# Rows of cumulative exponents for SSD heads: from selection matmuls to broadcast transfers, in a hybrid encoder

## The chip, the cores and the metric

The kernel runs on one core of one Trainium2 chip. The metric is the device time in microseconds; shown is the median of several executions. One further execution was recorded by the hardware profiler, and all durations come from that one.

## The reference

A two-layer encoder works on 16 meta tokens and 512 tokens of 2048 channels (528 positions). The first layer projects to SSD heads (Mamba-2, run in both directions) and to a convolution branch, gates both and projects back; the second is neighbourhood attention. The change lies in the SSD heads. Cut to one direction of them:

```python
A_cs = jnp.cumsum(A, axis=2)                     # per chunk and head, A = dt * -exp(A_log)
seg = A_cs[:, :, :, None] - A_cs[:, :, None, :]
Lmat = jnp.exp(jnp.where(tri, seg, -jnp.inf))
CB = jnp.einsum("bclgn,bcsgn->bclsg", Cc, Bc)
Y_diag = jnp.einsum("bclsgr,bcsgrp->bclgrp", CB[..., None] * Lmat, X)
...
Y_off = jnp.einsum("bclgn,bcgrpn->bclgrp", Cc, prev) * jnp.exp(A_cs)[..., None]
return (Y_diag + Y_off)
```

There are 32 heads of 64 channels in 8 groups; a group shares Bm and Cm. For each head and direction the kernel needs the row of cumulative exponents A_cs over all positions on many partitions at once: once as it is, to form the differences `seg` in a chunk, and once as exp(A_cs), to scale Cc for the part that comes from earlier chunks.

## The kernel before

Activations lie with channels on partitions and the 528 positions along the free dimension (L = 528, HL = 264). Positions are cut into NC = 6 chunks of CH = 88.

Every projection (`proj`) multiplies in three passes of 32-bit parts (high x high, high x low, low x high): for each of the 16 slices of the inner dimension 3 passes x 2 halves of 264 columns, 96 matmuls for a tile of 128 output channels. Weight panels of half a tile (128 x 8 x 128) are loaded on SP's queue (`load`), cast to the high part by ACT (L256, `wh`), subtracted to the low part by DVE (L259, `wl`); `raw`, `wh` and `wl` have three buffers each. The results lie in the PSUM tile `ps` (two buffers) and are taken out by DVE.

For each of the 8 groups, one or two further tiles of the convolution branch are projected (`glu_tile`), then six tiles: Bm (`bT`), Cm (`cT`), two of xs, two of z. After each projection `step()` lets two background generators go on: `ssd` of the group before, by a budget of 7000, and the 31-tap convolutions (`conv31`, on DVE, L447), by 6000. Each `yield` in a generator is the price of what it just emitted, and is taken off the budget. The tile framework then orders the instructions of each engine ahead of the run by a model of their times; the program order acts as priority. A fixed order of each engine results.

Ahead of the first group, `fc` is computed: 64 partitions (2 directions x 32 heads) x 528 cumulative exponents, from two scans (L514, L515). It is split into a high and a low part, both in `fhl` (128 partitions, L516 to L518). `sel` is a constant 128 x 64 of zeros and ones. dt and its relatives lie in slots that T and cq use afterwards (L486). Transposed columns of fc, dt and the decay to a chunk's end are in `fcol`, `dcol`, `wcol` (L535 to L542).

`ssd` of one group, in order: products of chunk and chunk (`pc`, L550) and their two masked forms (`cbs`); for each chunk the transposes (L563), the decayed inputs (`xd`) and the states (`st`, L573, into `pv`); the running states (L582, L585); then for each of two pairs of heads (`i`), for each head (`j`):

- for each direction, two matmuls (L598) with one column of `sel` spread over 128 columns select the row of fc for this head and put it on all 128 partitions in the PSUM tile `pf`;
- ACT forms T = relu(fcol - row) in six blocks of 88 columns (L601) and cq = exp(row) (L603), then T = exp(-T) (L604);
- DVE multiplies cq by cT (L605, L606); ACT scales T by dcol (L611), DVE multiplies by `cbs` (L612) and adds the directions (L614).

Both heads of a pair then go into `py` (L633), 64 matmuls from T, cq, xb and pv in six chunks; DVE takes it out (L637), multiplies by the gate (L638), and POOL's queue stores it to `yz_d` (L639). T and cq have two buffers each, so one pair of heads fills them. pc, pf and py share one slot of two PSUM banks (tag "big").

POOL's own work in this stage is small: the memsets at the edges of the convolution input `up` (L459, L460), one multiplication for each `glu_tile` (L656), the stores of `yz_d` and `cv_d`. Its instructions and the transfers on its queue run in order.

The next stage (from L706) projects 16 more tiles with `ln` beside it, then come the output projection, the attention layer and the last output projection, all with the same weight path.

Of the kernel before, what the change touches and what calls it, by code (L numbers as in the profile page):

```python
# [12 lines left out]
F32 = mybir.dt.float32  # L13
F32R = mybir.dt.float32r
AF = mybir.ActivationFunctionType
ALU = mybir.AluOpType

P = 128
# [5 lines left out]
L = NM + S  # L24
HL = L // 2
# [4 lines left out]
HPG = 4  # L30
HD = 64
CH = 88
NC = L // CH
NH = 32
# [48 lines left out]
def hybrid_encoder(ctx: ExitStack, tc: tile.TileContext, hT, win, wdt, wout, oin, oout, par, con,  # L83
                   rpb, out, dbg=None):
    nc = tc.nc
    dbg = dbg or {}

    cp = ctx.enter_context(tc.tile_pool(name="cp", bufs=1))
# [3 lines left out]
    dr = ctx.enter_context(tc.tile_pool(name="dr", bufs=1, space=bass.MemoryType.DRAM))  # L92
# [15 lines left out]
    def cn(n):  # L108
        lo, hi = CON[n]
        return cst[:, lo:hi]  # L110
# [4 lines left out]
    def h2(ap):  # L115
        return ap.rearrange("p (a b) -> p a b", a=2)

    yz_d = dr.tile([KT, P, L], F32, name="yz_d")
    cv_d = dr.tile([KT, P, L], F32, name="cv_d")
    pt_d = dr.tile([KT, P, L], F32, name="pt_d")  # L120
    yb_d = dr.tile([KT, P, L], F32, name="yb_d")
# [252 lines left out]
    with ExitStack() as c0:  # L374
        psb = c0.enter_context(tc.tile_pool(name="psb", bufs=1, space=bass.MemoryType.PSUM))
        sp = c0.enter_context(tc.tile_pool(name="sp", bufs=1))
        dp = c0.enter_context(tc.tile_pool(name="dp", bufs=1))
# [13 lines left out]
        for tag, n, bufs in (("T", 2, 2), ("T", 2, 2), ("cq", 2, 2), ("cq", 2, 2), ("xb", 4, 1), ("pv", 4, 1)):  # L391
            t = first_x if not raws else sp.tile([P, n, L], F32, name="hraw", tag=tag, bufs=bufs)
            for i in range(n):
                k = len(raws)
# [17 lines left out]
                if k >= 2:  # L412
                    nc.vector.tensor_tensor(ac, ac, raw, op=ALU.add)

        sel = cp.tile([P, 64], F32R, name="sel")
        nc.vector.tensor_copy(sel, cn("sel"))
        xp = [sp.tile([P, L + 4], F32, name=f"xp{i}") for i in range(2)]
        for t in xp:
            nc.gpsimd.memset(t[:, 0:2], 0.0)
# [2 lines left out]
        J = 64  # L422
# [64 lines left out]
        v, e, w, z, la, fc, wd, dexp = [t4[i // 2][:J, i % 2] for i in range(8)]  # L487
# [25 lines left out]
        nc.gpsimd.memset(rf[:, ::CH], 0.0)  # L513
        nc.vector.tensor_tensor_scan(fc[0:32], rf[0:32], la[0:32], 0.0, ALU.mult, ALU.add)  # L514
        nc.vector.tensor_tensor_scan(fc[32:64, ::-1], rf[32:64], la[32:64, ::-1], 0.0, ALU.mult, ALU.add)  # L515
        fhl = dp.tile([P, L], F32R, name="fhl")  # L516
        nc.scalar.activation(fhl[:J], fc, AF.Copy)
        nc.vector.tensor_tensor(fhl[J:], fc, fhl[:J].bitcast(F32), op=ALU.subtract)  # L518
        fc3 = fc.rearrange("p (c t) -> p c t", c=NC)
        wd3 = wd.rearrange("p (c t) -> p c t", c=NC)  # L520
        nc.vector.tensor_tensor(wd3[0:32], fc3[0:32, :, CH - 1:CH].to_broadcast([32, NC, CH]), fc3[0:32], op=ALU.subtract)
# [14 lines left out]
        for nm, src in (("fcol", fc), ("dcol", dt), ("wcol", wd)):  # L536
# [3 lines left out]
            t = dp.tile([CH, NC, 2, NH], F32, name=nm)  # L540
            nc.vector.tensor_copy(t.rearrange("p c r h -> p (c r h)"), pt[:CH, :NC * J])
            cols.append(t)  # L542
        fcol, dcol, wcol = cols

        def ssd(g, bT, cT, xs, zs):
            xb = sp.tile([CH, NC, 3 * P], F32, name="xb", tag="xb")
            pv = sp.tile([P, NC - 1, 2, 256], F32, name="pv", tag="pv")
            pc = psb.tile([P, 2, 512], F32, name="pc", tag="big")
# [11 lines left out]
            for c in range(NC):  # L560
                pt = psb.tile([P, 512], F32, name="pt", tag="sm", bufs=2)
                for i, src in enumerate((xs[0], xs[1], bT)):
# [11 lines left out]
                                 start=True, stop=True)  # L574
# [12 lines left out]
            for i in range(2):  # L587
                gs, cs = [], []
                for j in range(2):
                    hl = 2 * i + j  # L590
                    hd = HPG * g + hl
                    T = sp.tile([CH, 2, L], F32, name="T", tag="T", bufs=2)
                    cq = sp.tile([P, 2, L], F32, name="cq", tag="cq", bufs=2)
                    for d in range(2):
                        pf = psb.tile([P, 2, 512], F32, name="pf", tag="big")
                        jj = d * NH + hd
                        for n in range(2):
                            nc.tensor.matmul(pf[:, n, :HL], sel[:, jj:jj + 1].to_broadcast([P, P]),  # L598
                                             fhl[:, n * HL:(n + 1) * HL], start=True, stop=True)
                        for c in range(NC):  # L600
                            nc.scalar.activation(T[:, d, c * CH:(c + 1) * CH], pf[:CH, c // 3, (c % 3) * CH:(c % 3 + 1) * CH],  # L601
                                                 AF.Relu, bias=fcol[:, c, d, hd:hd + 1], scale=-1.0)
                        nc.scalar.activation(h2(cq[:, d]), pf[:, :, :HL], AF.Exp)  # L603
                    nc.scalar.activation(T, T, AF.Exp, scale=-1.0)  # L604
                    nc.vector.tensor_tensor(cq[:, 0, CH:], cq[:, 0, CH:], cT[:, CH:], op=ALU.mult)  # L605
                    nc.vector.tensor_tensor(cq[:, 1, :L - CH], cq[:, 1, :L - CH], cT[:, :L - CH], op=ALU.mult)  # L606
                    yield 1050
                    for d in range(2):
                        for c in range(NC):
                            sl = slice(c * CH, (c + 1) * CH)  # L610
                            nc.scalar.activation(T[:, d, sl], T[:, d, sl], AF.Copy, scale=dcol[:, c, d, hd:hd + 1])  # L611
                        nc.vector.tensor_tensor(T[:, d], T[:, d], cbs[d], op=ALU.mult)  # L612
                    yield 1900
                    nc.vector.tensor_tensor(T[:, 0], T[:, 0], T[:, 1], op=ALU.add)  # L614
                    yield 650
                    gs.append(T)
                    cs.append(cq)
                py = psb.tile([P, 2, 512], F32, name="py", tag="big")
                for c in range(NC):
                    sl = slice(c * CH, (c + 1) * CH)  # L620
                    terms = [[], []]
                    for j in range(2):
                        hs = slice((2 * i + j) * HD, (2 * i + j + 1) * HD)
                        terms[j].append((xb[:, c, hs], gs[j][:, 0, sl]))
                        if c > 0:
                            terms[j].append((pv[:, c - 1, 0, hs], cs[j][:, 0, sl]))
                        if c < NC - 1:
                            terms[j].append((pv[:, NC - 2 - c, 1, hs], cs[j][:, 1, sl]))
                    nt = len(terms[0])
                    for q in range(nt):  # L630
                        for j in range(2):
                            a, b = terms[j][q]
                            nc.tensor.matmul(py[j * HD:(j + 1) * HD, c // 3, (c % 3) * CH:(c % 3 + 1) * CH], a, b,  # L633
                                             start=(q == 0), stop=(q == nt - 1))
                ti = 2 * g + i
                y = xs[i]
                nc.vector.scalar_tensor_tensor(h2(y), h2(y), pr("dd", ti, ti + 1), py[:, :, :HL], op0=ALU.mult, op1=ALU.add)  # L637
                nc.vector.tensor_tensor(y, y, zs[i], op=ALU.mult)  # L638
                nc.gpsimd.dma_start(yz_d[ti], y)  # L639
                if ti == 0:  # L640
                    nc.scalar.activation(accy, y, AF.Square)
                else:
                    nc.scalar.activation(zs[i], y, AF.Square)
                    nc.vector.tensor_tensor(accy, accy, zs[i], op=ALU.add)
                yield 2100

        def step():
            pump(bgs, SB_)
# [57 lines left out]
    with ExitStack() as c1:  # L706
        psb = c1.enter_context(pool(name="psc", bufs=1, space=bass.MemoryType.PSUM))
        zb = c1.enter_context(pool(name="zbp", bufs=14))
        big = c1.enter_context(pool(name="big", bufs=16))
# [889 lines left out]
```

## Time and profile before

| | us |
|---|---|
| runs, median of 3 | 2636.21 (2633.34 to 2637.39) |
| profiled execution, its own time | 2635.41 |
| span of its instructions | 2633.6 |
| SSD stage, about | 130 to 1090 |
| one group (from one yz_d store to the same one of the next group) | 110.45 |

The span is what the profiler shows from the first instruction to the last; 1.8 us lie around it. Rows of the trace give start and duration in us from the span's start, the engine, the line and out<-in by the program's names. PE is TensorE's matmul, PEld its weight load, DVE VectorE, ACT ScalarE, POOL GpSimd, SP SyncE. What stands in square brackets behind an instruction is the idle time of the engine before it and what ended it. In the view of waits the numbers are the total in us, the times, the longest.

### The profile page before, as it was taken

What the parts mean: (1) busy time and instruction counts of PE and PEld (TensorE: products, weight loads), DVE (VectorE), ACT (ScalarE), POOL (GpSimd) and SP (SyncE); (2) the same over time, 40 slices, a digit from 0 to 9 for tenths busy, and PEclk for the clock granted to TensorE, in tenths of its full rate; (3) what the DMA queues carried; (4) which work ended last, traced back from release to release, by engine and by line L of the source; (5) the groups of instructions that cost most, each with busy time, mean ns of one, the idle gap of its engine ahead of it and who ended that gap; (6) DMA issues with size and microseconds to landing.
All of it is one profiled execution on the core that took longest, in us unless ns stands there. A gap on an engine that the chain in (4) does not pass through costs nothing.

```text
span 2633.6 us, 52655 instructions
## 1 busy us (share of the span) xinstructions
PE 2599.0 (99%) x21236; PEld 2485.8 (94%) x21236; DVE 2050.0 (78%) x3046; ACT 1417.3 (54%) x2636; POOL 363.2 (14%) x586
## 2 busy tenths in 40 slices
PE   8999999999999999999999999999999999999997
PEld 8999999999999999999999999999999987777797
DVE  6985967887686969997688888877777776666886
ACT  5366585666658566325554556633334355656543
POOL 0000000000000001100220312200000043443133
PEclk9999999999999999999999999999999999999999
DMA  4222223222222222533875877755555554443755
GB/s 173 98 76 93 81 77 97 81 94 74 92 85 76 88 90 92 177 108 112 266 234 166 296 217 229 239 159 157 157 156 148 151 144 134 135 131 117 232 171 166
DMA packets 147140, 373.40 MB, mean 142 GB/s; under 512 B 32704, under 2 KB 50784, under 8 KB 146896
## 3 DMA queue, kind: packets, MB, share of 16 engines
q1 hardware_dynamic: 121872, 290.09, 34.2%
q0 software_dynamic: 23008, 78.30, 11.2%
q8 instruction: 167, 2.74, 0.4%
q10 hardware_dynamic: 2016, 1.65, 0.2%
q14 instruction: 77, 0.63, 0.1%
HBM read 320.59 MB, written 49.38 MB: 140 GB/s over the span
## 4 chain that ended last, share of the span: by engine, by line
PE 88%; DVE 4%; ACT 4%; issue 2%; DMA 2%; POOL 0%; DVEq 0%; SPq 0%; ACTq 0%; POOLq 0%
PE ps L303 45%; PE pb L280 28%; PE ps L1179 6%; PE py L633 2%; PE po L1165 1%; PE st L573 1%; DVE a L447 1%; DVE wl L259 1%; PE pq L1116 1%; ACT wh L256 1%; ACT T L601 1%; ACT L603 1%; DMA srt<-h_d 1%; ACT sb L1122 1%; PE pa L1140 1%
## 5 line engine op out<-in xcount | busy, mean ns | idle before, releaser
L303 PE MATMUL ps<-rh,wh 128*128 128x264 f32 (+1 forms) x3520 | 730.7, 287 | 9.8 <-ACT rh L320 8.2
L303 PE MATMUL ps<-rh,wl 128*128 128x264 f32 (+1 forms) x3520 | 730.2, 287 | 0.0
L303 PE MATMUL ps<-rl,wh 128*128 128x264 f32 (+1 forms) x3520 | 725.8, 287 | 1.3 <-DVE rl L321 1.2
L256 ACT ACTIVATE wh<-raw 128x1024 fp32r<-128x1024 f32 (+1 forms) x349 | 369.1, 1057 | 528.9 <-PE ps L303 271.7
L259 DVE TENSOR_TENSOR wl<-raw,wh 128x1024 fp32r<-128x1024 f32 (+1 forms) x349 | 440.5, 1262 | 161.9 <-ACT wh L256 157.1
L303 PEld LDWEIGHTS ps<-rh,wh 128*128 128x128 f32 (+1 forms) x3520 | 549.3, 188 | 16.1 <-ACT rh L320 9.0
L303 PEld LDWEIGHTS ps<-rl,wh 128*128 128x128 f32 (+1 forms) x3520 | 546.5, 188 | 4.8 <-DVE rl L321 2.2
L303 PEld LDWEIGHTS ps<-rh,wl 128*128 128x128 f32 (+1 forms) x3520 | 548.9, 188 | 2.1
L280 PE MATMUL pb<-rh,wh 128*128 128x264 f32 (+1 forms) x1280 | 364.1, 285 | 1.0 <-ACT wh L256 1.0
L280 PE MATMUL pb<-rh,wl 128*128 128x264 f32 (+1 forms) x1280 | 363.1, 284 | 0.0
L280 PE MATMUL pb<-rl,wh 128*128 128x264 f32 (+1 forms) x1280 | 363.0, 284 | 0.0
L447 DVE SCALAR_TENSOR_TENSOR a<-up,prm,a 128x528 f32<-128x528 f32 x464 | 343.2, 770 | 2.3 <-ACT a L442 0.9
L280 PEld LDWEIGHTS pb<-rh,wh 128*128 128x128 f32 x1280 | 241.2, 188 | 1.8 <-ACT wh L256 1.2
L280 PEld LDWEIGHTS pb<-rl,wh 128*128 128x128 f32 x1280 | 241.1, 188 | 0.0
L280 PEld LDWEIGHTS pb<-rh,wl 128*128 128x128 f32 x1280 | 240.4, 188 | 0.1
L280 PE MATMUL pb<-ta,wh 128*128 128x264 f32 (+1 forms) x1280 | 236.1, 283 | 0.4 <-ACT wh L256 0.4
L280 PEld LDWEIGHTS pb<-ta,wh 128*128 128x128 f32 x1280 | 198.2, 188 | 0.7 <-ACT wh L256 0.6
L256 ACT ACTIVATE wh<-wy 128x1024 fp32r<-128x1024 f32 x109 | 115.5, 1059 | 138.2 <-PE pb L280 98.5
L280 PE MATMUL pb<-ta,wl 128*128 128x264 f32 (+1 forms) x640 | 182.0, 285 | 2.6 <-DVE wl L259 2.4
L259 DVE TENSOR_TENSOR wl<-wy,wh 128x1024 fp32r<-128x1024 f32 x109 | 138.1, 1268 | 58.7 <-ACT wh L256 58.5
L256 ACT ACTIVATE wh<-wb 128x1024 fp32r<-128x1024 f32 x80 | 84.7, 1059 | 99.6 <-PE pb L280 75.3
L280 PEld LDWEIGHTS pb<-ta,wl 128*128 128x128 f32 x640 | 120.3, 188 | 3.4 <-DVE wl L259 3.4
(389 smaller groups left out, 4119.1 us busy)
## 6 DMA issues: line engine op xcount, KB each, us to landing
raw<-win SPq DMA_DIRECT2D x192, 512.0 KB, 3.7
raw<-oin SPq DMA_DIRECT2D x84, 512.0 KB, 4.5
raw<-wout SPq DMA_DIRECT2D x40, 512.0 KB, 5.5
wb<-oin SPq DMA_DIRECT2D x22, 512.0 KB, 3.9
wy<-oin SPq DMA_DIRECT2D x22, 512.0 KB, 3.4
wy<-oin POOLq DMA_DIRECT2D x22, 512.0 KB, 7.3
raw<-oout SPq DMA_DIRECT2D x20, 512.0 KB, 4.9
srt<-h_d POOLq DMA_DIRECT2D x38, 264.0 KB, 5.3
```

The source lines that it names most:

```text
L256: nc.scalar.activation(wh, raw, AF.Copy)
L259: nc.vector.tensor_tensor(wl, raw, wh.bitcast(F32), op=ALU.subtract)
L280: nc.tensor.matmul(o, w[:, k, :], u[:, lo:lo + n], start=(new and k == 0 and j == 0), stop=(k == KH - 1 and j == 2), skip_group_check=not new)
L303: nc.tensor.matmul(ps[:M, n, :N], w[:, k, :], u[:, lo + n * N:lo + (n + 1) * N], start=(kk == 0 and j == 0), stop=(kk == KT - 1 and j == 2))
L447: nc.vector.scalar_tensor_tensor(a, u[:, j:j + L], wv(j), a, op0=ALU.mult, op1=ALU.add)
L573: nc.tensor.matmul(st[:, :nd * 256], xb[:, c, 256:], xd[:, d0:d1].rearrange("p r x -> p (r x)"), start=True, stop=True)
L601: nc.scalar.activation(T[:, d, c * CH:(c + 1) * CH], pf[:CH, c // 3, (c % 3) * CH:(c % 3 + 1) * CH], AF.Relu, bias=fcol[:, c, d, hd:hd + 1 ...
L603: nc.scalar.activation(h2(cq[:, d]), pf[:, :, :HL], AF.Exp)
L633: nc.tensor.matmul(py[j * HD:(j + 1) * HD, c // 3, (c % 3) * CH:(c % 3 + 1) * CH], a, b, start=(q == 0), stop=(q == nt - 1))
L1116: nc.tensor.matmul(pqs[a, w][:, :n], x[hs, w * P:(w + 1) * P], y[hs, st:st + n], start=(j == 0), stop=(j == 2))
L1122: nc.scalar.activation(sv, sv, AF.Exp, bias=mx, scale=-1.0, accum_out=self.sm[a][:, w:w + 1])
L1179: nc.tensor.matmul(ps, w[:, k, :], u[:, lo:lo + S], start=(kk == 0 and j == 0), stop=(kk == KT - 1 and j == 2))
```

## The change

The rows of fc and of exp(fc) are written to DRAM once (`f_d`), and each head's T and cq are filled by transfers that read one row of f_d for all partitions (a step of 0 over partitions). ACT then computes the Relu in place in T, and the exponential of cq is no longer computed per head. `sel`, `fhl`, the matmuls into `pf` and the copies that split fc go. The loads of the first pair of heads (`rows(g, 0)`) are emitted at the start of a group's `ssd`, those of the second (`rows(g, 1)`) behind the first pair's matmuls into py. All are on POOL's queue. The price at the end of the first pair is 5100 in place of 2100.

```diff
+    f_d = dr.tile([2, 2 * NH, L], F32, name="f_d")
...
-        sel = cp.tile([P, 64], F32R, name="sel")
-        nc.vector.tensor_copy(sel, cn("sel"))
...
-        fhl = dp.tile([P, L], F32R, name="fhl")
-        nc.scalar.activation(fhl[:J], fc, AF.Copy)
-        nc.vector.tensor_tensor(fhl[J:], fc, fhl[:J].bitcast(F32), op=ALU.subtract)
+        nc.gpsimd.dma_start(f_d[0], fc)
+        ef = e
+        nc.scalar.activation(ef, fc, AF.Exp)
+        nc.gpsimd.dma_start(f_d[1], ef)
...
+        def rows(g, i):
+            out = []
+            for j in range(2):
+                hd = HPG * g + 2 * i + j
+                T = sp.tile([CH, 2, L], F32, name="T", tag="T", bufs=2)
+                cq = sp.tile([P, 2, L], F32, name="cq", tag="cq", bufs=2)
+                for k, t in enumerate((T, cq)):
+                    s = f_d[k, hd]
+                    nc.gpsimd.dma_start(t, bass.AP(tensor=s.tensor, offset=s.offset,
+                                                   ap=[[0, t.shape[0]], [NH * L, 2], [1, L]]))
+                out.append((T, cq))
+            return out
+
         def ssd(g, bT, cT, xs, zs):
+            rw = rows(g, 0)
...
-                    T = sp.tile([CH, 2, L], F32, name="T", tag="T", bufs=2)
-                    cq = sp.tile([P, 2, L], F32, name="cq", tag="cq", bufs=2)
+                    T, cq = rw[j]
                     for d in range(2):
-                        pf = psb.tile([P, 2, 512], F32, name="pf", tag="big")
-                        jj = d * NH + hd
-                        for n in range(2):
-                            nc.tensor.matmul(pf[:, n, :HL], sel[:, jj:jj + 1].to_broadcast([P, P]),
-                                             fhl[:, n * HL:(n + 1) * HL], start=True, stop=True)
                         for c in range(NC):
-                            nc.scalar.activation(T[:, d, c * CH:(c + 1) * CH], pf[:CH, c // 3, (c % 3) * CH:(c % 3 + 1) * CH],
-                                                 AF.Relu, bias=fcol[:, c, d, hd:hd + 1], scale=-1.0)
-                        nc.scalar.activation(h2(cq[:, d]), pf[:, :, :HL], AF.Exp)
+                            sl = slice(c * CH, (c + 1) * CH)
+                            nc.scalar.activation(T[:, d, sl], T[:, d, sl], AF.Relu, bias=fcol[:, c, d, hd:hd + 1], scale=-1.0)
...
+                if i == 0:
+                    rw = rows(g, 1)
...
-                yield 2100
+                yield 2100 if i else 5100
```

## The prediction

> **What bounds the kernel now.** I read the page first, then the busy time by stage, then the chain of waits inside the stage that is changed, then each engine's waits there.
>
> ```profile
> span 2633.6 us, 52655 instructions
> ...
> PE 2599.0 (99%) x21236; PEld 2485.8 (94%) x21236; DVE 2050.0 (78%) x3046; ACT 1417.3 (54%) x2636; POOL 363.2 (14%) x586
> ...
> PE 88%; DVE 4%; ACT 4%; issue 2%; DMA 2%; POOL 0%; DVEq 0%; SPq 0%; ACTq 0%; POOLq 0%
> ```
>
> TensorE is busy for 99% of the span, and 88% of the chain that ended last is its matmuls. A busy PE can still be a waiting one, so the stages come next. The SSD heads run from about 130 to 1090 us; the rows are busy us and instruction counts of each engine, granted clock, DMA share, GB/s.
>
> ```profile
> core 0: us, PE busy (x) PEld busy (x) DVE busy (x) ACT busy (x) POOL busy (x), PEclk, DMA share, GB/s
> 130.00:1090.00 960.00, 957.83 (x8285) 926.32 (x8284) 755.23 (x1035) 597.74 (x1319) 51.53 (x79) 1.00 0.28 91
> 1090.00:1800.00 710.00, 707.02 (x5808) 705.96 (x5807) 583.30 (x810) 355.60 (x493) 109.72 (x190) 1.00 0.63 197
> 1800.00:2633.00 833.00, 812.13 (x6171) 733.39 (x6169) 608.82 (x1064) 400.49 (x740) 198.66 (x295) 0.99 0.53 154
> ```
>
> In the SSD stage PE is idle for 960 - 957.83 = 2.2 us, at full clock, while DVE has 205 us of room, ACT 362, POOL 908 and the DMA engines 72% of theirs. Work taken off PE here should shorten the stage by its own length, and the next stage (3.0 us of PE idle in 710) passes the gain on, because PE is the limit there too. The selection matmuls and their readers, by tile:
>
> ```profile
> L601 ACT ACTIVATE T<-pf,fcol x384: 308/331/383, 150.0 to 1047.6; 88x88 f32<-88x88 f32 x192
> L598 PEld LDWEIGHTS pf<-fhl,sel x128: 185/188/192, 148.9 to 1045.9; 128*128 128x128 f32 x128
> L598 PE MATMUL pf<-fhl,sel x128: 278/284/389, 149.0 to 1046.0; 128*128 128x264 f32 x128
> ```
>
> A matmul's 284 ns is latency; what counts is its place in the stream, which the chain of waits gives. One group, between the two halves of its heads:
>
> ```profile
> 404.52 28.71 PE ps L303 x236
> 433.24 2.44 PE py L633 x60
> 435.68 3.49 PE ps L303 x27
> 439.17 0.26 PE pf L598 x2
> ...
> 467.86 2.60 PE py L633 x62
> ```
>
> 236 projection matmuls of the same 264 columns in 28.71 us are 0.122 us each, and two selection matmuls take 0.26, the same pace.
>
> **The change part by part.** *Removed from PE:* 32 heads x 2 directions x 2 halves = 128 matmuls x 0.122 = **15.6 us**, all between 149 and 1046 us where PE has no spare time. They also leave the one two-bank PSUM slot ("big") that pf shared with pc and py, and with it the waits that this slot made:
>
> ```profile
> PE pf L598 <- ACT cq L603: 1.4, 4, 0.3
> PE py L633 <- ACT cq L603: 0.6, 3, 0.2
> ```
>
> The 1.4 us before pf go with pf. The 0.6 before py I leave in, since py will still wait for a cq.
>
> *ACT:* 64 exponentials of cq go. The 384 Relus stay but read SBUF in place of PSUM, a form that is not in the trace; the nearest row that reads and writes T in SBUF in blocks of 88 columns is L611.
>
> ```profile
> L611 ACT ACTIVATE T<-T,dcol 88x88 f32<-88x88 f32 x384 | 103.4, 371 | 0.5
> L601 ACT ACTIVATE T<-pf,fcol 88x88 f32<-88x88 f32 x384 | 91.5, 334 | 20.0 <-PE pf L598 20.0
> L603 ACT ACTIVATE cq<-pf 128x528 f32<-128x528 f32 x64 | 39.8, 623 | 0.3
> ```
>
> By busy time that is -39.8 for cq and 103.4 - 91.5 = +11.9 for the Relus (bounds 0 and 11.9), so 28 us less on ACT, and its 20.0 us of waiting for pf go as well. None of it counts directly, for ACT has 362 us of room. One exponential of 64 x 528 (ef) stands where the copy to fhl was, and on DVE the subtraction L518 and the copy to sel go: nothing on the path.
>
> *The transfers:* each head loads a T of 88 x 2 x 2112 B = 363 KB and a cq of 528 KB; 32 heads make 28,512 KB, 29.2 MB. Over the stage's 960 us that adds 30 GB/s to its 91, so by the ratio the DMA share goes from 0.28 to about 0.37. The weight loads share the engines; that they have slack shows in what ACT waits for before it casts a weight panel:
>
> ```profile
> ACT wh L256 <- PE ps L303: 141.3, 50, 5.3
> ```
>
> It waits for PE to give a panel back, and not for a transfer: the casts run ahead by the three buffers of wh. A panel feeds 48 matmuls, 48 x 0.122 = 5.9 us, so a delay of several us on ACT or on a weight load is absorbed. Without that cover, each late us would be a us of PE.
>
> *POOL* issues the 128 loads and two stores. The rows for one issue of 128 rows, and for one of 256 pieces (128 partitions x 2):
>
> ```profile
> L721 POOL DMA_DIRECT2D xc<-cv_d x16: 536/536/552, 1067.9 to 1186.7; - x16
> ```
>
> ```profile
> L770 POOL DMA_DIRECT2D accy<-vqk_d x1: 720/720/720, 1667.6 to 1667.6; - x1
> ```
>
> T has 176 pieces and cq 256, so I take 0.72 us: 128 x 0.72 = 92 us on an engine that is busy for 52 of 960. Queued behind the four loads of a pair stand the store of yz_d and the multiplication for sg:
>
> ```profile
> 437.53 0.55 POOL L639 DMA_DIRECT2D yz_d<-cv  x1 [21.13 <-DVE cv L638]
> 466.23 1.32 POOL L656 TENSOR_TENSOR sg<-sg,rs 128x528 f32<-128x528 f32 x1 [28.15 <-ACT sg L655]
> ```
>
> Between them POOL sits idle for 28 us, so 4 x 0.72 = 2.9 us of issues hide; the late yz_d store is read only in the next stage.
>
> *The added wait.* The loads of a group's first pair of heads start when its ssd starts, long before py needs them. Those of the second pair (rows(g, 1)) can only start once py of the first pair has let T and cq go, at 435.7 in this group, and py of the second pair ran at 467.86. What must fit into these 32 us is: landing, Relus, exponentials, products. How fast a broadcast from DRAM lands is not in the trace; the nearest rows (KB each, us to landing), and the busiest stretch of loads on POOL's queue:
>
> ```profile
> xc<-cv_d POOLq DMA_DIRECT2D x16, 264.0 KB, 4.9
> ...
> o_d<-o SPq DMA_DIRECT2D x16, 256.0 KB, 2.0
> ...
> bt<-rpb SPq DMA_DIRECT2D x30, 132.5 KB, 3.6
> ```
>
> ```profile
> 1067.00:1081.00 14.00, 14.00 (x117) 14.00 (x116) 14.00 (x21) 3.84 (x4) 6.94 (x13) 1.00 0.94 332
> ```
>
> The quick end: 332 GB/s less the 91 of the stage are 241 GB/s; a pair of heads (1782 KB, 1.825 MB) then needs 7.6 us + 2.0 (o_d, the shortest landing of a tile) = 9.6, the first T about 2.0 + 1.5 = 3.5. So T is there at 439 to 440, and all four tiles by 446. The slow end is bt, which reads overlapping pieces of one small region, as a broadcast does: 3.6 - 2.0 = 1.6 us for 132.5 KB, 85 GB/s. The first T lands after 6.4 us and the last cq after 23.5. I take the quick end: xc is the nearest row in queue, length of a row (2112 B) and size, and bt's 3.6 us also holds its place behind other loads. Before, the second head's Relu and the last product with cq stood here:
>
> ```profile
> 454.03 1.41 ACT L601 ACTIVATE T<-pf,fcol 88x88 f32<-88x88 f32 x6
> ```
>
> ```profile
> 459.04 0.62 DVE L606 TENSOR_TENSOR cq<-cq,cv 128x440 f32<-128x440 f32 x1 [0.89 <-ACT cq L603]
> ```
>
> With 446 the transfers are ahead of both. What stays uncertain is the order on PE and ACT, which is fixed ahead of the run: where a load lands later than that order allows for, PE stands at py. For this I put in 0.25 us for each of 8 second pairs, +2 (from below: 0; from above: see the rivals). The longer pause (yield 5100) moves the second pair by 3000 of the 7000 that a step is given. The same store one group earlier:
>
> ```profile
> 327.08 0.54 POOL L639 DMA_DIRECT2D yz_d<-cv  x1 [21.17 <-DVE cv L638]
> ```
>
> A group takes 437.53 - 327.08 = 110.45 us and has 8 steps, so the pause is 3000/7000 x 13.8 = 5.9 us. The next group's first py comes one group after 433.24, at 543.7, which is 73 us after this group's last one ends (470.5): the shift costs nothing.
>
> *The start.* f_d must be written and read back before the first Relu at 150.0, and the slots of T and cq are held until the last transposes of their contents:
>
> ```profile
> 131.91 0.80 PE pt L539 x12
> ```
>
> From 132.7 there are 17 us for 9.6 of loads: hidden, at 23.5 (the slow end) 6 us late, once.
>
> **Sum:** -15.6 - 1.4 + 2.0 = **-15.0 us**. The profiled execution took 2635.41 us (span 2633.6 and 1.8 around it); 2620.4 against it. The median of the runs is 0.8 higher, so the forecast is **2621 us** (-0.6%).
>
> **The rivals.**
>
> *Given back at py (no change):* the loads of each second pair come 2 us later than the fixed order has room for; 8 x 2 = 16 us eat the gain: 2637. For it: the second pair's chain is tight (its selection matmul ran at 439.17, 3.5 us after py let T go). Against: the pair's work on ACT gets shorter by four exponentials, about 2.5 us.
>
> *Broadcast reads crawl (slower):* if loads from two rows of DRAM go at bt's 85 GB/s, the second T lands at 435.7 + 2.0 + 15.0 = 452.7 and the last cq at 459.2. An order made for the quick end can place the second head's Relu as early as 446, where ACT then stands for 6.7 us and py behind it; at the old place (454.03) it would not wait. Between the two I take 4 us for each second pair, 32 in all in place of the 2 of the sum: 2651. It decides from 20.3 us of loss (15.0 + 0.2%), which is 2.5 us for each second pair. Against: the stage's DMA engines are 72% free.
>
> *Queued behind a wait on POOL (slower):* POOL stands for long stretches at the memsets of up.
>
> ```profile
> POOL up L459 <- DVE a L447: 395.0, 12, 58.8
> ```
>
> A load ordered behind one would be up to 58.8 us late; at 25 us in two groups 2671. Against: at 435.7 the memset of this group is long past.
>
> *Starved descriptors:* in this trace a DVE that is busy for all of 14.00 us (1067 to 1081) leaves POOL's issues at 536 ns. If an issue did have to wait for one DVE instruction, at most the 1.2 us of a weight subtraction, the first T of each second pair would be 1.2 us later: 8 x 1.2 = 9.6, 2631. [...]
>
> **How the numbers follow.** 0.2% is 5.3 us, about what a measurement of this kernel can tell from no change. Forecast 0.69 (its own range 2613 to 2628: the quick end without any new wait is 2619, and 24 us of PE idle in the later stages, 3.0 + 20.9, may shift by a quarter either way under a new order); given back at py 0.13; slow broadcasts 0.11; POOL's queue 0.03; starved descriptors 0.04, half of it inside 0.2%. Faster 0.69 + 0.02 = 0.71, same 0.13 + 0.02 = 0.15, slower 0.14. The range runs from 2613 to 2637, the forecast's low end to the case in which all is given back; it leaves out the two slower cases and a few hundredths of tails.
>
> **What would show it.** PE should have 128 instructions fewer, and the SSD stage end 15 us sooner, with PE idle still near 2 us. Loads of T should land in 4 to 6 us and of cq in 5 to 9; ten or more speaks for slow broadcasts. Waits of PE at py beyond 8 us in all, or of ACT's Relu for T's transfer beyond some 20, show the gain going back. POOL's issues above 1 us speak for the starved descriptors. The forecast is wrong if a later stage takes the gain (PE idle after 1090 growing beyond 24 us), or if the weight casts begin to wait for transfers.

## The result and the profile after

| | before | after |
|---|---|---|
| runs, median | 2636.8 us (4 runs) | 2671.41 us (4 runs) |
| ratio, 95% interval | | 1.0138 [1.0125, 1.015] |
| span of the profiled execution | 2633.6 us | 2669.1 us |
| mean granted clock of TensorE | 0.998 | 0.989 |

The changed kernel is 1.4% slower. The forecast was 2621 us, the range ended at 2637.

The lines of the changed kernel are shifted: the projections are L304, the Relus L610, the exponentials L611, the scalings L618, the cq products L612 and L613, the copies to xb L578, xd L582, st L587, py L640, the row loads L553. First the page of the changed kernel, its span, busy times and the chain that ended last:

```profile
span 2669.1 us, 52424 instructions
...
PE 2599.6 (97%) x21108; PEld 2485.9 (93%) x21108; DVE 2052.3 (77%) x3044; ACT 1390.7 (52%) x2564; POOL 410.7 (15%) x652
...
PE 71%; ACT 9%; DVE 7%; issue 6%; DMA 6%; POOL 1%; SPq 0%; DVEq 0%; POOLq 0%; ACTq 0%
PE ps L304 30%; PE pb L281 27%; PE ps L1188 6%; DMA T<-f_d 3%; ACT T L610 3%; DVE a L446 2%; DVE wl L260 2%; ACT wh L257 1%; ACT T L618 1%; PE py L640 1%; PE st L587 1%; PE po L1174 1%; ACT L611 1%; PE pq L1125 1%; ACT T L611 1%
```

PE has its 128 instructions fewer, yet it is busy as long as before (2599.6 against 2599.0 us), and the span is 35.5 us longer. So PE is idle some 35 us more, and the matmuls that are left take longer by about what the 128 took before. Of the chain PE now has 71% in place of 88; ACT, issue and DMA have gained 4 to 5 points each, DVE 3. The stages, as shown of before (busy us and counts by engine, granted clock, DMA share, GB/s):

```profile
core 0: us, PE busy (x) PEld busy (x) DVE busy (x) ACT busy (x) POOL busy (x), PEclk, DMA share, GB/s
130.00:1090.00 960.00, 923.93 (x7892) 892.64 (x7891) 731.49 (x999) 563.95 (x1239) 87.51 (x127) 0.98 0.36 113
1090.00:1800.00 710.00, 704.82 (x5776) 703.68 (x5775) 585.55 (x816) 347.63 (x484) 116.71 (x202) 1.00 0.64 201
1800.00:2669.00 869.00, 848.76 (x6465) 769.87 (x6463) 633.11 (x1093) 415.52 (x756) 200.54 (x297) 0.99 0.53 154
```

Nearly all of the new idle time is in the SSD stage: PE is idle there for 960 - 923.93 = 36.1 us in place of 2.2, at a clock of 0.98. In the later stages it is 5.2 and 20.2 us (before 3.0 and 20.9). The waits of PE, ACT and DVE (total us, times, longest):

```profile
PE st L587 <- DVE xd L582: 22.5, 10, 4.1
PE py L640 <- ACT T L618: 8.5, 3, 3.1
...
PE py L640 <- DVE T L621: 4.1, 3, 2.8
```

```profile
ACT T L610 <- DMA T<-f_d: 43.6, 16, 4.7
```

```profile
DVE cq L612 <- DMA cq<-f_d: 60.4, 28, 6.5
```

Before, PE waited 0.6 us at py and not at all at st. The larger part is now at **st**, in the first half of a group's ssd, and not at the py of the second pair. How a wait for T gets to st is to be seen in the order of ACT behind a group's last py, whose slots let the next group's loads go (changed kernel, POOL, ACT, DVE and PE by time):

```profile
361.20 1.49 POOL L553 DMA_DIRECT2D T<-f_d  x2 [29.50 <-PE py L640]
362.69 1.45 POOL L553 DMA_DIRECT2D cq<-f_d  x2
```

```profile
362.47 0.64 ACT L652 ACTIVATE zt<-cv 128x528 f32<-128x528 f32 x1 [6.01 <-DVE cv L647]
366.43 0.37 ACT L610 ACTIVATE T<-T,fcol 88x88 f32<-88x88 f32 x1 [3.32 <-DMA T<-f_d]
366.71 1.04 ACT L257 ACTIVATE wh<-raw 128x1024 fp32r<-128x1024 f32 x1
367.66 3.21 ACT L610 ACTIVATE T<-T,fcol 88x88 f32<-88x88 f32 x12
370.88 1.28 ACT L664 ACT_TABLE_LOAD   x1
372.18 0.65 ACT L664 ACTIVATE sg<-sg 128x528 f32<-128x528 f32 x1
372.73 0.47 ACT L578 ACTIVATE xb<-pt 88x384 f32<-88x384 f32 x1
```

```profile
373.23 1.25 DVE L582 TENSOR_TENSOR xd<-xb,wcol 88x256 f32<-88x256 f32 x1 [0.73 <-ACT xb L578]
```

```profile
374.53 0.70 PE L587 MATMUL st<-xd,xb 88*128 88x256 f32 x2 [1.37 <-DVE xd L582]
```

Before, the two stood the other way round. ACT copied xb first, and the first Relu came 9 us later, behind a matmul into pf (kernel before, ACT, the same group):

```profile
359.88 0.49 ACT L564 ACTIVATE xb<-pt 88x384 f32<-88x384 f32 x1 [4.19 <-PE py L633]
...
369.03 1.41 ACT L601 ACTIVATE T<-pf,fcol 88x88 f32<-88x88 f32 x6
```

Now the first Relu stands in front of xb in ACT's order. Its T was asked for at 361.20 and is there at 366.43, 5.2 us later. Everything behind it (a weight cast, xb, and through xb the xd of DVE) is late by what ACT stood, and PE waits at st. The landing times of all loads (KB each, median us from issue to landing):

```profile
raw<-win SPq DMA_DIRECT2D x192, 512.0 KB, 3.6
...
cq<-f_d POOLq DMA_DIRECT2D x32, 528.0 KB, 8.2
T<-f_d POOLq DMA_DIRECT2D x32, 363.0 KB, 6.3
```

The second effect is the clock. Three stretches of 4 us around one of the waits at py (same columns as the stages):

```profile
345.00:349.00 4.00, 4.00 (x35) 4.00 (x34) 0.63 (x1) 3.97 (x6) 0.00 (x0) 1.00 0.02 4
349.00:353.00 4.00, 1.02 (x9) 0.81 (x7) 2.71 (x4) 4.00 (x17) 0.00 (x0) 1.00 0.38 131
353.00:357.00 4.00, 3.93 (x22) 3.85 (x23) 3.08 (x4) 3.45 (x9) 0.00 (x0) 0.67 0.00 0
```

PE is idle for 3 us of the second stretch, and in the third it is busy but gets through 22 matmuls where the first stretch had 35: the clock is 0.67 on the mean of 4 us. So this wait cost more than its own 3 us.

### The profile page after: what moved, and what is told of

Read it like the earlier page. It is cut to its first block, busy times and chain, and to the rows that moved or that the text cites. A ratio compares the mean times of both kernels' runs of the same rounds, so it can differ in the third digit from the quotient of the medians.

```text
span 2669.1 us, 52424 instructions
## 1 busy us (share of the span) xinstructions
PE 2599.6 (97%) x21108; PEld 2485.9 (93%) x21108; DVE 2052.3 (77%) x3044; ACT 1390.7 (52%) x2564; POOL 410.7 (15%) x652
## 4 chain that ended last, share of the span: by engine, by line
PE 71%; ACT 9%; DVE 7%; issue 6%; DMA 6%; POOL 1%; SPq 0%; DVEq 0%; POOLq 0%; ACTq 0%
PE ps L304 30%; PE pb L281 27%; PE ps L1188 6%; DMA T<-f_d 3%; ACT T L610 3%; DVE a L446 2%; DVE wl L260 2%; ACT wh L257 1%; ACT T L618 1%; PE py L640 1%; PE st L587 1%; PE po L1174 1%; ACT L611 1%; PE pq L1125 1%; ACT T L611 1%
## 5 line engine op out<-in xcount | busy, mean ns | idle before, releaser
L304 PE MATMUL ps<-rh,wh 128*128 128x264 f32 (+1 forms) x3520 | 731.4, 288 | 10.4 <-ACT rh L321 8.2
L304 PE MATMUL ps<-rh,wl 128*128 128x264 f32 (+1 forms) x3520 | 732.9, 289 | 1.3 <-DVE wl L260 1.3
L304 PE MATMUL ps<-rl,wh 128*128 128x264 f32 (+1 forms) x3520 | 730.6, 288 | 0.2
L304 PEld LDWEIGHTS ps<-rh,wh 128*128 128x128 f32 (+1 forms) x3520 | 553.1, 190 | 14.6 <-ACT rh L321 8.8
L304 PEld LDWEIGHTS ps<-rh,wl 128*128 128x128 f32 (+1 forms) x3520 | 552.5, 190 | 5.0 <-DVE wl L260 2.0
L304 PEld LDWEIGHTS ps<-rl,wh 128*128 128x128 f32 (+1 forms) x3520 | 551.2, 190 | 3.3 <-DVE rl L322 1.0
L610 ACT ACTIVATE T<-T,fcol 88x88 f32<-88x88 f32 x384 | 103.0, 354 | 45.9 <-DMA T<-f_d 43.6
```

Source lines behind the costliest of these rows:

```text
L304: nc.tensor.matmul(ps[:M, n, :N], w[:, k, :], u[:, lo + n * N:lo + (n + 1) * N], start=(kk == 0 and j == 0), stop=(kk == KT - 1 and j == 2))
L610: nc.scalar.activation(T[:, d, sl], T[:, d, sl], AF.Relu, bias=fcol[:, c, d, hd:hd + 1], scale=-1.0)
```

## The experiments

The theory after the result: ACT and DVE, whose order is fixed ahead, stand at rows that land 5 to 13 us after py, and what is behind them makes PE late. Rivals: the longer pause, the engine time of the new forms, contention with the weights, POOL's issues or queue, the loads' traffic itself. Eighteen kernels were run; each ratio is against the kernel before in the same series, with its 95% interval.

### What the transfers cost: e1, e8, e3

e1 reads one fixed row for all heads:

```diff
+        rowt = dp.tile([P, L], F32, name="rowt")
+        s0 = f_d[1, 0]
+        nc.gpsimd.dma_start(rowt, bass.AP(tensor=s0.tensor, offset=s0.offset, ap=[[0, P], [1, L]]))
...
-                    nc.gpsimd.dma_start(t, bass.AP(...))
...
-  nc.scalar.activation(T[:, d, sl], T[:, d, sl], AF.Relu, ...)
+  nc.scalar.activation(T[:, d, sl], rowt[:CH, sl], AF.Relu, ...)
...
```

The products of cq read rowt too. The loads that it leaves out are 64 in all, 32 of T and 32 of cq.

> Leaves out the 64 transfers per direction of rows to heads: every head's Relu and cq product read one row that is loaded once, so the selection matmuls are gone and no head waits for a transfer. Theory A (loads land later than the fixed order of ACT and PE has room for, and in-order ACT makes PE late): 2615 to 2628 us, PE idle in the SSD stage near 2 us, clock near 1.00. Theory B (the new order or the longer pause makes PE stand, whatever the loads do): 2650 or more. Theory C (29 MB more traffic slow the weight panels): 2615 to 2628 as in A.

Measured: 2625.3 us, ratio 0.996 [0.9949, 0.9972]. The same instructions without the transfers are 1.4% + 0.4% = 1.8%, some 47 us, faster than the changed kernel: **all of the loss hangs on the transfers**. The stage and the page of e1:

```profile
130.00:1090.00 960.00, 952.90 (x8282) 924.25 (x8281) 777.24 (x1061) 579.36 (x1255) 48.42 (x81) 1.00 0.28 93
```

```profile
PE 2584.2 (98%) x21108; PEld 2473.4 (94%) x21108; DVE 2050.2 (78%) x3044; ACT 1395.6 (53%) x2568; POOL 362.7 (14%) x589
```

PE is busy for 2599.0 - 2584.2 = 14.8 us less than before, which is the selection matmuls; it is idle 7.1 us of the stage in place of 2.2, so that about 10 us are left. Of the 7.1, 3.9 are waits at st behind DVE's xd and 2.9 at py behind DVE's T.

e8 makes each load twice in a row:

```diff
+                    for _ in range(2):
                         nc.gpsimd.dma_start(t, bass.AP(...))
```

> The changed kernel with each row transfer made twice, the second behind the first, which doubles the time to landing and the bytes. Theory A and D: the landings of a pair come some 10 us later than now, partly allowed for by the order; 2685 to 2760. If the landing time does not matter (theory B): below 2680.

Measured: 2724.99 us, ratio 1.0342 [1.0327, 1.0358]. The second loads cost another 2.0%, 54 us, about what the first cost. PE's waits at st grow to 31.5 us, and 26.3 us come up at a new place, ps behind DVE's sg. ACT and DVE now stand about twice as long in the stage:

```profile
ACT T L611 <- DMA T<-f_d: 100.9, 17, 10.1
```

```profile
DVE cq L613 <- DMA cq<-f_d: 106.2, 23, 12.0
```

e3 undoes the longer pause:

```diff
-                yield 2100 if i else 5100
+                yield 2100
```

> The changed kernel with the price of the pause between the pairs back at 2100. Theory A: within 6 us of the changed kernel's 2671, or slower, since the loads have less time. Theory B (the pause): most of the loss goes, 2645 or less. Theory C: as A.

Measured: 2670.91 us, ratio 1.0129 [1.0107, 1.0151]: the pause does nothing that can be measured.

### The order held by hand, with two buffers: e2, e5, e6, e11

e2 puts each first pair's Relus on ACT behind the last state copy to pv; e5 puts also the first pair's cq products on DVE behind the last xd; e6 puts every head's cq products behind its sum of T; e11 is e5 with the loads issued by SP.

```diff
+                    with tc.issue_after(lastpv.ins) if i == 0 else ExitStack():     # e2, e5, e6, e11
                         ... the Relus
+                    with tc.issue_after(lastxd.ins) if i == 0 else ExitStack():     # e5, e11
                         ... the products of cq and cT
-                    nc.gpsimd.dma_start(t, bass.AP(...))
+                    nc.sync.dma_start(t, bass.AP(...))                              # e11
```

> The changed kernel, with the first pair's Relus queued on ACT behind the last copy of the group's states, so that they can't stand in front of the copies for xb. Theory A: the waits of PE at st (22.5 us) fall below 5 and the time to 2640 to 2655, with the waits at py (12.6 us) left. Theories B and C: 2665 to 2675, since neither loads nor pause change.

Measured: 2661.52 us, 1.0091 [1.0074, 1.0108]. It is some 10 us faster than the changed kernel, but the waits at st did not go (23.7 us). The reading was that with ACT out of the way it is DVE that stands in front of xd, at cq. That is what e5 takes away.

> The second run's edit, and the first pair's two products with cq queued on DVE behind the group's last xd as well. Theory D (both in-order queues count: with the Relus held, DVE stands at the first pair's cq, and cmu, cml and xd behind it are late): PE's waits at st go from 23.7 us to below 6 and the time to 2630 to 2645. If DVE's waits for cq cost nothing, as an idle engine's would: 2658 to 2665.

Measured: 2651.26 us, 1.0058 [1.0043, 1.0073], between its two expectations. All of PE's waits of the stage, from e5's view of waits:

```profile
PE py L642 <- ACT T L620: 13.2, 3, 5.3
PE py L642 <- DVE T L623: 10.1, 4, 3.5
PE ps L304 <- ACT wh L257: 1.8, 2, 1.0
```

Those at st are gone, which confirms the path through xb and xd. What is left is the second pairs' chain from the landing to py, 23.3 us, more than the 12.6 us of the changed kernel there. Each of these seven waits is in front of two matmuls of py that stand 5 to 11 us ahead of the other 62 in PE's order, and so need a T sooner than the rest.

> As the run before, with the cq products of both pairs on DVE behind the sum of their head's T, so that DVE never stands at a cq ahead of other work. Theory D: st as in the run before, waits at py below 10 us, 2628 to 2642. What stays above the run without transfers (2625) is the second pair's T, which can't be loaded before py of the first pair. If only the first pair counted: the same as the run before within 3 us.

Measured: 2653.33 us, 1.0065 [1.0049, 1.0082]: the waits at py fall to 10.7 us, but others of 7.6 us for weight casts come up, and the time stays within 3 us of e5, the second of its expectations.

> e5 with the row loads issued by SP in place of POOL. If the landing time comes from POOL's queue or its issuing (0.73 to 0.76 us each): landing of T falls from 6.9 to 4 us or less, and 2630 to 2643 us. If it is the four loads' own traffic: landing 6 us or more and 2647 to 2656 us, or a little slower where SP's own loads of weights stand behind them.

Measured: 2646.46 us, 1.0051 [1.0035, 1.0067]. Between the two expectations: some 5 us at most are POOL's here, and the intervals of e5 and e11 overlap. The engines go on standing at rows (ACT 48.9 us, DVE 31.6), so the queue is not the main cause.

### More buffers: e4, e15, and four misses

e4 has four buffers of T; rsa and the tiles tagged st move to a later pool for the room. e15 has the move alone.

```diff
-                T = sp.tile([CH, 2, L], F32, name="T", tag="T", bufs=2)
+                T = sp.tile([CH, 2, L], F32, name="T", tag="T", bufs=4)
...
-    rsa = cp.tile([P, L], F32, name="rsa")
+    lp = ctx.enter_context(pool(name="lp", bufs=1, side="right"))
+    rsa = lp.tile([P, L], F32, name="rsa")
```

> The changed kernel with four buffers of T in place of two (room from two later tiles that are placed elsewhere while the SSD stage runs); cq keeps two. The T of a pair is then loaded while the pair before is at work. Theory A: ACT's waits for the transfer of T (43.6 us) fall below 8 and the time to 2620 to 2640, the rest being waits for cq. Theories B and C: 2665 to 2675.

> The changed kernel with two buffers, but with rsa and the tiles tagged st moved to the later pool, as in all kernels with more buffers. If the room by itself does nothing: 2666 to 2676 us as the changed kernel. If part of e4's 25 us came from it: 2645 to 2662 us.

Measured: e4 2645.83 us, 1.0034 [1.002, 1.0048]; e15 2668.9 us, 1.0122 [1.0097, 1.0147]. The room does nothing, the two further buffers of T bring some 23 us. That is less than was expected (2620 to 2640 us): ACT still stands at T for 19.1 us and DVE at cq for 34.9, and PE waits 15.6 us at st.

Then buffers and a held order were put together. e7 is e6 with four T, e12 is e5 with four T, e9 has three of T and of cq, the order of e5 for the first pairs, and each second head's work behind the first's.

> The run before with four buffers of T as well, so that ACT never waits for a T in front of other work. Theory D: within 6 us of the run without transfers (2619 to 2631), faster than the kernel before. If the transfers cost something besides the standing queues (traffic, POOL's issues): 2635 or more.

> Three buffers each of T and of cq in place of two (the first head of a pair then has its rows while the pair before is still in use; rsa and the tiles tagged st are moved to a later pool for the room), the order of e5 for the first pairs, and each second head's Relus behind the first head's scalings, its cq products behind the first head's sum. Theory (the engines that work in a fixed order stand at rows that land late): 2618 to 2634 us, faster than before; PE's idle time between 130 and 1090 us below 15 us, its waits at st and py together below 10 us, ACT's waits for T below 20 us. Rival (the order itself costs, whatever the rows do, as the kernel with four T and late products suggests): 2645 to 2666 us with ACT still standing at T for 30 us and more.

> Four buffers of T (e4) with the order of e5 for the first pairs. If the two gains add (e4 took 25 us off the changed kernel, e5 20 us): 2624 to 2634 us, waits at st gone, ACT's waits for T below 20 us. If the early T loads make the order run ahead of what lands, as in e7: 2645 to 2668 us, with ACT's waits for T above 30 us.

Measured: e7 2666.2 us, 1.0109 [1.0091, 1.0127]; e9 2662.17 us, 1.0107 [1.0091, 1.0122]; e12 2661.4 us, 1.0098 [1.0081, 1.0115]. None of the three gave what the theory hoped for. e9 and e12 came out as the other expectation had it, with ACT standing at T for 62.3 and 35.7 us. The two gains do not add; e7 is slower than e6 and e4, and e12 slower than e5 and e4. For e12 the order of instructions says why: as only the first pairs were held, and a second pair needs no slot of the first any more, all 24 Relus of the second pair stand directly behind py, in front of xb. ACT and POOL of e12 by time:

```profile
350.45 1.49 POOL L552 DMA_DIRECT2D T<-f_d  x2 [16.41 <-PE py L641]
```

```profile
358.12 5.55 ACT L610 ACTIVATE T<-T,fcol 88x88 f32<-88x88 f32 x21 [5.45 <-DMA T<-f_d]
...
379.30 0.47 ACT L577 ACTIVATE xb<-pt 88x384 f32<-88x384 f32 x1
```

ACT takes up work long before PE wants it, as soon as the slot is free, and stands there at a load that has just been issued. e13 therefore holds the second pairs too, behind the first pair's last scaling, and e14 is e13 on SP's queue.

```diff
+                    with tc.issue_after(lasts.ins if i else lastpv.ins):
                         ... the Relus
+                    with tc.issue_after(lastT.ins):
                         ... the products of cq and cT, behind the head's sum of T
```

> Four buffers of T, so that a pair's T is loaded one pair ahead, and now an order in which no engine can stand at rows: the first pair's Relus behind the last state copy, the second pair's behind the first pair's last scaling, and every head's cq products behind its sum of T. Theory (the engines' fixed order stood at late rows; e7, e9 and e12 failed since the second pair's Relus were put in front of xb): 2620 to 2632 us, faster than before; ACT's waits for T in 130 to 1090 us below 10 us, PE's idle time there below 15 us, no stretch of low clock besides one or two. Rival (the landing itself, or the traffic of the loads, costs whatever the order): 2640 to 2660 us.

> e13 with the row loads on SP's queue in place of POOL's, among the loads of the weights. If e13's order covers the landing, the queue no longer matters: within 5 us of e13. If SP's loads of weights now stand behind waiting row loads: PE's waits for casts grow and it is 5 us or more above e13.

Measured: e13 2687.22 us, 1.0186 [1.0168, 1.0204]; e14 2672.02 us, 1.0136 [1.0111, 1.016]. e13 is slower than the changed kernel, though ACT stands at no T in the stage any more. PE waits 28.1 us at py and 12.9 for weight casts. Held so tightly, all of a group's T work begins only behind the last pv, and PE's order has the second pair's py close behind the first's (PE of e13, by time):

```profile
323.63 0.32 PE L643 MATMUL py<-T,xb 88*64 88x88 f32 x4
...
331.01 0.34 PE L643 MATMUL py<-T,xb 88*64 88x88 f32 x2 [1.48 <-ACT T L616]
...
338.73 0.38 PE L643 MATMUL py<-T,xb 88*64 88x88 f32 x1 [3.67 <-DVE T L619]
```

The second py begins 7 us behind the end of the first, and PE waits in it. The kernel before left 26 us, from 435.7 to its first two matmuls of the second py:

```profile
461.47 0.37 PE L633 MATMUL py<-T,xb 88*64 88x88 f32 x2
```

So e13 tells little on landing, for it put one bad order in the place of another. e14 went against both of its expectations: it is 15 us faster than e13, with 19.9 us of waits at py against 28.1 and 8.0 us of DVE's waits for cq against 14.1. So with this order SP's queue does help; whether by a sooner landing or by its issuing was not separated. A cure had to leave ACT's order alone.

### The floor and the cure: e10, e16, e17, e18

e10 is e1 with e5's order.

> e1 (no transfers per head, one row read by all; leaves out the loads of the heads' own rows) with the order of e5 for the first pairs. It asks where the 5 us went that e1 did not show of the 15.6 us of selection matmuls. If the first pair's Relus and cq products in front of xb and xd cost them even with the rows at hand: 2617 to 2622 us, the waits at st gone. If they come from the second pairs or from elsewhere: 2624 to 2627 us as in e1.

Measured: 2624.56 us, 0.9969 [0.9956, 0.9982], the same as e1. Without transfers the order held by hand brings nothing: the waits at st are gone, but those at py are 8.1 us in place of 2.9. So the 5 us of the 14.8 that e1 doesn't show are waits of PE behind ACT and DVE; the held order moves them and doesn't end them, and why they came up is open.

e16 to e18 load rows into tiles of their own, which are free again once the Relus (or the products) have read them. The next pair's rows of T can then be asked for while this pair's py is still to come, and the Relus, which write T, wait for T's slot as in e1. e16 stages T's rows (two tiles tr) and puts the cq products behind the sum of T; e17 stages T's rows alone; e18 stages both rows, one tile each, and holds nothing.

```diff
-                T = sp.tile([CH, 2, L], F32, name="T", tag="T", bufs=2)
+                T = sp.tile([CH, 2, L], F32, name="tr", tag="tr", bufs=2)
...
-                    T, cq = rw[j]
+                    R, cq = rw[j]
+                    T = sp.tile([CH, 2, L], F32, name="T", tag="T", bufs=2)
...
-  nc.scalar.activation(T[:, d, sl], T[:, d, sl], AF.Relu, ...)
+  nc.scalar.activation(T[:, d, sl], R[:, d, sl], AF.Relu, ...)
```

> T's rows are loaded into two tiles of their own (tr), read by the Relus, which write T as e1's do; a tr is free once its Relus are done, so the next pair's rows are asked for before py. cq's rows are loaded as in the changed kernel, but its products stand behind their head's sum of T. The order on ACT is nearly that of e1. Theory (it is the standing at late rows in a fixed order, and nothing else): 2624 to 2634 us, ACT's waits for rows in 130 to 1090 us below 8 us, PE's idle time there below 14 us. Rival (the loads cost something beside, or the late products do): 2640 us or more with ACT hardly waiting.

> e16 with the cq products left where the changed kernel has them. What remains over e16 is DVE's standing at cq: 2630 to 2645 us, DVE's waits for cq 30 us or more. If DVE's waits don't matter to PE: as e16.

> Both rows of a head loaded into tiles of their own, one buffer each (more don't fit), so that a head's rows are asked for as soon as the head before has read its own; nothing held. If the lead is long enough (a head's work is 15 us or more, a landing 4 to 6 us when two are in flight): 2622 to 2632 us, waits of ACT and DVE for rows below 20 us together. If not: 2635 to 2650 us with such waits above 30 us.

Measured: **e16 2625.65 us, 0.9964 [0.9952, 0.9976]; e17 2633.18 us, 0.999 [0.9981, 0.9999]; e18 2632.48 us, 0.9988 [0.9979, 0.9997].** e16 has every transfer of the changed kernel and is as fast as e1, which has none of the 64. Its stage, loads, and ACT's wait for rows:

```profile
130.00:1090.00 960.00, 951.64 (x8245) 920.67 (x8244) 768.75 (x1053) 579.48 (x1255) 101.32 (x142) 1.00 0.39 122
```

```profile
cq<-f_d POOLq DMA_DIRECT2D x32, 528.0 KB, 6.8
tr<-f_d POOLq DMA_DIRECT2D x32, 363.0 KB, 7.0
```

```profile
ACT T L610 <- DMA tr<-f_d: 3.9, 1, 3.9
```

The rows of T land no sooner (7.0 us), but they are asked for in time. One request and the Relus that read it, by time (e16, POOL and ACT):

```profile
323.84 0.75 POOL L552 DMA_DIRECT2D tr<-f_d  x1 [0.96 <-ACT T L610]
```

```profile
346.15 5.04 ACT L610 ACTIVATE T<-tr,fcol 88x88 f32<-88x88 f32 x19 [1.87 <-PE py L641]
```

The request follows the Relu that has read the tile before, and the row has 22 us to land. What ACT waits for is py, which frees T's slot. PE is idle for 8.4 us of the stage, and the clock is back at 1.00. This settles it: neither the traffic nor POOL's issuing costs more than the intervals allow, some 3 us; the loss was the standing at late rows. e17 gives the shares. From e15 (the changed kernel with the tiles moved) to e17, T's rows asked for early bring 1.3%, some 35 us; from e17 to e16, cq's products out of the way bring 0.26%, some 7 us, although DVE's waits for cq in e17 are longer than ACT's for T in the changed kernel:

```profile
DVE cq L612 <- DMA cq<-f_d: 70.9, 27, 9.4
```

e18 ends between its two expectations: with one tile for each row the lead is short, and 38.3 us of waits for rows (ACT 7.5, DVE 30.8) are left. Two tiles for both rows weren't run, and neither was e16 with its loads on SP's queue.

## Why the prediction was wrong, point by point

**Right.** The selection matmuls are worth what was worked out: 15.6 forecast, 14.8 us of busy time in e1. The Relus' new form was bounded at 103.4 us and takes 103.0:

```profile
L610 ACT ACTIVATE T<-T,fcol 88x88 f32<-88x88 f32 x384 | 103.0, 354 | 45.9 <-DMA T<-f_d 43.6
```

POOL's issue was put at 0.72 us:

```profile
L553 POOL DMA_DIRECT2D T<-f_d x32: 746/756/796, 123.7 to 1047.7; - x32
L553 POOL DMA_DIRECT2D cq<-f_d x32: 718/729/747, 128.7 to 1049.2; - x32
```

The DMA share came to 0.36 (0.37 forecast), the pause costs nothing that can be measured (e3), and the weights' panels still land in 3.6 us. One count was wrong without touching the sum: the loads are 64, not 128, since one transfer holds both directions, and POOL is busy 47.5 us longer (410.7 against 363.2) and not 92.

**The step that failed is "the added wait"**, put in at 0.25 us for each second pair, 2.0 in all. From e1 to the changed kernel it measures some 47 us, the slower clock behind the waits included. Three things in that step and beside it were wrong.

1. *The place.* It looked at the second pairs alone and held that a group's first loads start "long before py needs them". So they do, but py is not what reads them first. The Relus stand in front of xb in ACT's order, and their landing is paid at st: 22.5 us of waits there against 12.6 at py, and gone in e5. For the second pairs, too, the place was off: the step let py run at 467.86, but two of its matmuls stood at 461.47, so that the room was 26 us and not 32, and nearly all of PE's waits at py in the changed kernel are in front of these two.
2. *The comparison.* The quick end was nearly right: 3.5 us were forecast for the first T, and 5.2 measured in the group shown; 9.6 us for all four tiles, and 11.3 in the pair ahead of it, where the last cq held DVE up to 339.45 (POOL and DVE of the changed kernel):

```profile
328.18 1.51 POOL L553 DMA_DIRECT2D T<-f_d  x2 [16.96 <-PE py L640]
```

```profile
339.45 0.62 DVE L612 TENSOR_TENSOR cq<-cq,cv 128x440 f32<-128x440 f32 x1 [0.71 <-DMA cq<-f_d]
```

   But the step compared these times with the places where the Relus stood before, which the pf matmuls on PE had set. With pf gone nothing held them there: ACT's order took them up as soon as their slot was free, and a load that is issued only at that moment is late even when it lands in 5 us. The text said that an order could be fixed too early, and gave that a chance in the rivals, but it put near nothing into the sum.
3. *The cover.* "a delay of several us on ACT or on a weight load is absorbed", by the casts that run ahead, and "ACT has 362 us of room". Both are true, of casts (PE's waits for weight panels in the stage of the changed kernel are 1.0 us, at ps behind DVE's wl) and of averages (ACT is busy for 563.95 us of 960). xb is not covered by either: in the group shown st follows it by 1.8 us (372.73 to 374.53), with xd between, and it stands in the same queue behind the late Relu.

**Not foreseen** was the clock: 44 us at half speed between 231 and 1559 us, 41 of them in the SSD stage, where the kernel before had none. PE is busy 15.4 us longer than in e1 (2599.6 against 2584.2), which has the same matmuls and a clock of 1.00 in the stage against 0.98 here. That is about what the change had saved.

**The rivals.** "Given back at py" had the right kind of wait and gave 16 us; there are 12.6 us of waits at its place, which was the smaller one. "Broadcast reads crawl" had the sign (2651), by a mechanism that isn't there: four tiles land in some 11 us, near the quick end. "Queued behind a wait on POOL" did not come: POOL still stands at up (332.3 us in the stage), but the longest single wait of ACT for a T is 4.7 us and of DVE for a cq 6.5, so no row was held up by tens of us. All 335 transfers on POOL's queue did land in the order of their issue. "Starved descriptors" fell: the issues take 0.73 to 0.76 us, and e16 with the same issues is as fast as e1. Two of the signs named in the forecast did turn up: more than 8 us of waits at py (12.6), more than 20 of ACT at T (43.6). A third was touched, PE's idle time after 1090 us at 25.4 (24 named).

## What to carry to other kernels

When work on the bound engine that also paced the others is replaced by a transfer, ask where the reader of the transfer will stand in its engine's order and what is queued behind it; the idle share of that engine says nothing on this. Load into tiles that the first reader sets free, so that the request goes out well ahead (22 us in e16), rather than into the buffers that the last reader holds. An order held by hand at one place can move the standing to the next one: e2, e7, e9, e12 and e13 each show it.

## What was not expected of the hardware

TensorE's clock fell after quite short waits. Counted over the trace of the changed kernel from 140 to 2600 us, all seven pauses of PE of 2.5 us or more (2.78 to 4.11) were followed by a stretch at half clock of 3.4 or 6.8 us, beginning 2.0 to 4.3 us after the pause began. Of pauses between 1.6 and 2.5 us two (1.76 and 1.81) were followed by one and four (1.63 to 2.47) were not, and of shorter ones none was. All nine stretches begin at whole multiples of 3.413 us from one another, and the shortest pause ahead of one was 1.76 us, about half of that.

Four loads that each spread two rows of 2112 B over 88 or 128 partitions, 1782 KB in all, land in 9.8 to 12.9 us beside the weights' loads (the changed kernel, all pairs but the first). The quick end of the forecast, worked out from other transfers of this kernel that read each byte once, was 9.6; against that estimate the loads, which read the same few KB of memory 88 or 128 times over, took 0.2 to 3.3 us more.
